# A decoder layer's attention softmax: the bias addition writes negated logits and returns the negated row maximum

## The chip, the cores and the metric

The kernel runs on one core of a Trainium2 chip. A core has five engines with an instruction queue each: TensorE (PE, matrix multiply, with its weight loads shown as PEld), VectorE (DVE), ScalarE (ACT), GpSimd (POOL) and SyncE (SP, which issues most DMAs here). They run side by side and wait for each other through semaphores. The metric is the time of one execution on the device, in microseconds (us).

## What is computed

One layer on 512 tokens of width 1024, in float32: a normalization, one combined projection to q, k, v, two recurrent inputs and two gates, differential attention with 8 heads, a gated linear recurrence beside it, a merge, an output projection, and a squared-ReLU MLP of width 4096. The change is in the softmax of the attention:

```python
logits = jnp.einsum('bqhcd,bkhcd->bhcqk', q_blk, k).astype(jnp.float32) * scale
logits = logits + bias[None, :, None]
logits = jnp.where(rel >= 0, logits, -jnp.inf)
p = jax.nn.softmax(logits, axis=-1)
attn = p[:, :, 0] - lam * p[:, :, 1]
return jnp.einsum('bhqk,bkhe->bqhe', attn.astype(v.dtype), v)
```

Each head has two maps (c = 0 and 1). Each gets a softmax of its own, and the second is subtracted, weighted with lam.

## The kernel before

Every float32 product is made of three matmuls on a high and a low part of each operand. So each weight tile is loaded by DMA (`wraw`), cast by ACT to its high part (`whi`), and DVE subtracts to get the low part (`wlo`). The projection products go to PSUM tiles called `acc`, those of the attention to five shared PSUM tiles called `at`.

The attention runs as 32 steps, 8 heads by 4 blocks of 128 queries; step s has head s // 4 and block i = s % 4, and n = 128 (i + 1) keys. For one step, in this order:

- `logits`: PE makes the two maps' logits (L595), two matmuls each, into two `at` tiles.
- `soft_a`: DVE adds the bias `toep` (which also holds the causal mask) to each map and takes the row maximum in the same instruction. This is one `tensor_tensor_reduce` per map, followed by a small read of the accumulator into `mx`. DVE then makes `nm`, which is `mx` times -1, for both maps at once. ACT takes the exponential of each map with `nm` as bias and sums the rows.
- `soft_b`, one step later: DVE makes the reciprocal `rc` of a row sum, a factor `r2`, and combines the two maps in place (`pe<-pe,r`).
- `turn`, two steps later: PE transposes the combined map, a block of 128 at a time (`ident,pe`, L631). ACT casts the result to its high part `pt`, and DVE subtracts to get the low one (`turn_low`).
- `av`, after every second block: PE multiplies `pt` with `v`.

After each step the loop fills in projection work of the next pair of heads (`qkv_pair`), or of the gates at the end: `acc` matmuls on PE, casts `whi` and squares on ACT, `wlo`, `qn` and `ss` on DVE, and the turning of q and k on PE (`ident,qn`, L529).

The instructions of DVE, ACT and POOL are chained by hand in the order of the program (the wrapper `InOrder`, whose calls all carry line L69). PE in this stage is not: there the framework's scheduler decides how the attention's matmuls and the projections' matmuls follow each other, from its own estimate of when an operand is ready. After the attention come the recurrent branch, the merge and the MLP, which the change does not touch.

Of the kernel before, what the change touches and what calls it, by code (L numbers as in the profile page):

```python
# [13 lines left out]
F32 = mybir.dt.float32  # L14
F32R = mybir.dt.float32r
I32 = mybir.dt.int32
AF = mybir.ActivationFunctionType
ALU = mybir.AluOpType
# [3 lines left out]
P = 128  # L22
# [17 lines left out]
def tile_block(ctx: ExitStack, tc: tile.TileContext, x, w_in, w_rga, w_rgx, w_pa, w_pr, w_o,  # L40
# [7 lines left out]
    sm = ctx.enter_context(tc.tile_pool(name="sm", bufs=4))  # L48
# [28 lines left out]
    V, A, G, T = InOrder(nc.vector), InOrder(nc.scalar), InOrder(nc.gpsimd), nc.tensor  # L77
# [338 lines left out]
    toep = {}  # L416
# [18 lines left out]
    def work(name):  # L435
        return wk.tile([P, S], F32, tag="pe", name=name, bufs=5)
# [144 lines left out]
    def attention(fills, qks, vs, pads):  # L581
        st = {}

        def place(s):
            return s // NT, s % NT
# [12 lines left out]
        def soft_a(s):  # L598
            h, i = place(s)
            n = P * (i + 1)  # L600
            lg = st[s]
            mx = sm.tile([P, 2], F32, tag="mx", name="mx")
            pe = [work("pe") for _ in range(2)]
            for c in range(2):
                V.tensor_tensor_reduce(out=pe[c][:, :n], in0=lg[c][:, :n], in1=toep[h][:, 384 - P * i:512], scale=1.0,
                                       scalar=-3e38, op0=ALU.add, op1=ALU.max, accum_out=mx[:, c:c + 1])
            nm = sm.tile([P, 2], F32, tag="nm", name="nm")
            V.tensor_scalar(out=nm, in0=mx, scalar1=-1.0, scalar2=None, op0=ALU.mult)
            if i == 0:
                st["sums", h] = sm.tile([P, 2, NT], F32, tag="sums", name="sums", bufs=3)  # L610
            sums = st["sums", h]
            for c in range(2):
                A.activation(pe[c][:, :n], pe[c][:, :n], AF.Exp, bias=nm[:, c:c + 1], accum_out=sums[:, c, i:i + 1])
            st[s] = pe

        def soft_b(s):
# [78 lines left out]
        for s in range(NH * NT):  # L695
            h, i = place(s)
            at(s, logits, s)
            at(s, soft_a, s)
            at(s + 1, soft_b, s)
            at(s + 2, turn, s)  # L700
            at(s + 2, turn_low, s)
            if i % 2 == 1:
                at(s + 3, av, s)
            if i == 3:
                at(s + 3, post_a, h)
                at(s + 4, post_b, h)
                at(s + 5, post_c, h)
                at(s + 7, post_d, h)
        for h in range(2, NH):
            at(NT * h - 3, toep_in, h)  # L710
        order = [toep_in, post_c, post_b, av, post_a, turn, logits, soft_a, soft_b, post_d, turn_low]
        for step in sorted(acts):
            j = step // (2 * NT)
# [322 lines left out]
    def task(engine, us, go, after=(), land=None):  # L1036
        t = Task(engine, us, go, [x for x in after if x is not None], AFTER.get(engine, 0.0) if land is None else land)
        for x in t.after:
            x.then.append(t)
        plan.append(t)  # L1040
        return t
# [315 lines left out]
    last_of_chunk, pe, queue, seq = {}, None, {}, []  # L1357
# [3 lines left out]
    def bank_task(key, us, go, after, fresh):  # L1361
        if fresh:
            seq.append(key)
            if len(seq) > 8:
                after = list(after) + queue[seq[-9]]
        else:
            after = list(after) + queue.get(key, [])
        return task("PE", us, go, after)
# [8 lines left out]
    def product_go(o, pairs, u, fresh):  # L1377
        kind, a, p = o
        b, f = (kind, a, BANK.get(p, "Y")), FORM[p]
        split_y = kind == "dn" and a[0] == 3 and b[2] == "Y"  # L1380

        def go():
            if fresh:
                banks[b] = (*banks.get(b, ()), psum("acc")) if split_y else psum("acc")
            hi, lo = units[o]
            if fresh and o in STEADY and u.start == 0:
                first = banks[b][0] if split_y else banks[b]
                x = forms[2 * a[0]][:, 0, f] if kind == "dn" else h2[:, 0, 0, 0:2]
                I.matmul(first[:, :384], hi[:, 0, :P], x.rearrange("p h s -> p (h s)")[:, :384], start=True, stop=True)
            for v in range(u.start, u.stop):  # L1390
                d = banks[b][v][:, :256] if split_y else banks[b][:, 256 * v:256 * v + 256]
                for z, i in enumerate(pairs):
                    for e, (l, r) in enumerate(((hi, 0), (hi, 1), (lo, 0))):
                        act = h2[:, r, i, ACT8[p]] if kind != "dn" else forms[2 * a[0] + i // 2][:, r, f, i % 2]
                        I.matmul(d, l[:, i, P * v:P * v + P], act, start=fresh and z == e == 0 and (v == 0 or split_y),
                                 stop=i == 3 and e == 2, skip_group_check=True)
        return go

    def plain_go(o, half):
        kind, a, p = o  # L1400
        oc, kc = int(p[1]) % 2, int(p[1]) // 2

        def go():
            hi, lo = units[o]
            if kc == half == 0:
                for u in range(2):
                    banks[kind, a, oc, u] = psum("acc")
            for m in range(4 * half, 4 * half + 4):
                u, i = (m // 4, m % 4) if kc else (m % 2, m // 2)
                for e, (l, r) in enumerate(((hi, 0), (hi, 1), (lo, 0))):  # L1410
                    I.matmul(banks[kind, a, oc, u], l[:, i, P * u:P * u + P], h2[:, r, i, 2 * kc:2 * kc + 2], start=kc == i == e == 0, stop=kc == 1 and i == 3 and e == 2)
        return go

    for kind, a, p, pairs in steps:
        o = kind, a, p
        if kind == "pl":
            oc, kc = int(p[1]) % 2, int(p[1]) // 2
            for half in range(2):
                pe = task("PE", 2.73, plain_go(o, half), (pe, lows[o]))
# [4 lines left out]
            if p == "b3":  # L1424
                pe = task("PE", 0.46, norm_go, (pe, norm_split))
# [21 lines left out]
        for u in (slice(0, 1), slice(1, 2)) if split_y else (slice(0, 2),):  # L1447
            key = (*b, u.start) if split_y else b
            pe = bank_task(key, 2.73 * len(pairs) / 4 * (u.stop - u.start) / 2 + 0.17 * (fresh and o in STEADY and u.start == 0), product_go(o, pairs, u, fresh), [pe, *after], fresh)
# [158 lines left out]
```

## Time and profile before

| | us |
|---|---|
| median of 3 runs | 840.35 |
| lowest and highest run | 839.96, 840.93 |
| the profiled execution's own time | 840.35 |
| its span, first to last instruction | 838.6 |
| attention stage, about | 55 to 285 |
| from the recurrent branch on, about | 285 to 838.6 |

The granted clock of TensorE is 1.0 throughout. In the profile's rows, L69 is the line of the wrapper, so instructions of DVE, ACT and POOL are told apart by their tiles: `pe<-at,toep` is the bias addition with its maximum, `mx` the accumulator read, `nm<-mx` the sign change, `pe<-pe,nm` the exponential, `pe<-pe,r` the combining step. "PEld ... [0.45 <-X]" means that the engine stood idle 0.45 us before that instruction and that X ended the wait; "issue" means that the profile names none.

### The profile page before, as it was taken

Reading aid. Unit: us, or ns where it says so; the run is one execution under the profiler, and the core shown is the slowest. Engines: PE = TensorE matmul, PEld = TensorE weight load, DVE = VectorE, ACT = ScalarE, POOL = GpSimd, SP = SyncE. Lnnn points to the kernel's source line nnn. Section 1 sums busy time; section 2 is a strip of 40 time slices with the busy share of each in tenths; the row PEclk is TensorE's granted clock in tenths of the full one; section 3 lists DMA queues with packets and bytes.
Section 4 is the critical chain, followed back from the end, with each engine's and each line's share of the span. In section 5 each row is a group of like instructions: output and inputs, shape, how many; then the busy total and the mean of one; then the engine's idle time right before and its main releaser. Section 6 shows DMA issues by size and latency. Waiting matters only on the chain.

```text
span 838.6 us, 14384 instructions
## 1 busy us (share of the span) xinstructions
PE 832.1 (99%) x5686; PEld 765.0 (91%) x5686; DVE 654.8 (78%) x1077; ACT 478.9 (57%) x753; POOL 104.0 (12%) x132
## 2 busy tenths in 40 slices
PE   9999999999999999999999999999999999999998
PEld 7899999999988887888888888899999999999998
DVE  6776788887877336879766767899989969977996
ACT  7445466555665334685763345774488448645851
POOL 0041231413201101111111000000000000000000
PEclk9999999999999999999999999999999999999999
DMA  6357332433322346667657662355655576556563
GB/s 202 124 153 217 91 110 66 103 123 91 88 77 76 88 138 196 195 189 209 182 170 179 197 253 76 101 151 145 209 151 151 151 256 170 144 164 200 151 168 110
DMA packets 41172, 126.10 MB, mean 150 GB/s; under 512 B 4992, under 2 KB 9800, under 8 KB 41104
## 3 DMA queue, kind: packets, MB, share of 16 engines
q1 hardware_dynamic: 31152, 92.65, 33.6%
q0 software_dynamic: 9952, 32.53, 18.1%
q8 instruction: 45, 0.74, 0.3%
q14 instruction: 23, 0.19, 0.1%
HBM read 102.05 MB, written 11.05 MB: 135 GB/s over the span
## 4 chain that ended last, share of the span: by engine, by line
PE 87%; DVE 5%; DMA 4%; ACT 2%; issue 1%; SPq 0%; ACTq 0%; DVEq 0%
PE acc L69 37%; PE acc L139 14%; PE acc L140 13%; PE acc L141 13%; DMA wraw<-in_w_in_dram 3%; PE at L595 2%; DVE wlo L69 2%; PE at L139 2%; PE at L141 2%; PE at L140 2%; PE at L631 1%; ACT whi L69 1%; PE at L529 1%; DVE pe L69 1%; PE at L668 1%
## 5 line engine op out<-in xcount | busy, mean ns | idle before, releaser
L69 ACT CAST whi<-raw 128x1024 fp32r<-128x1024 f32 x109 | 112.2, 1049 | 93.8 <-DVE raw L69 34.1
L69 DVE TENSOR_TENSOR wlo<-wraw,whi 128x1024 fp32r<-128x1024 f32 (+2 forms) x86 | 96.9, 1148 | 73.7 <-ACT whi L69 73.6
L69 PE MATMUL acc<-us,whi 128*128 128x256 f32 x900 | 153.8, 277 | 0.0
L69 PE MATMUL acc<-h,whi 128*128 128x256 f32 (+1 forms) x851 | 153.7, 285 | 0.0
L69 DVE TENSOR_TENSOR wlo<-raw,whi 128x1024 fp32r<-128x1024 f32 x109 | 131.0, 1218 | 21.0 <-ACT whi L69 20.9
L69 PEld LDWEIGHTS acc<-us,whi 128*128 128x128 f32 x900 | 135.8, 188 | 0.0
L69 PEld LDWEIGHTS acc<-h,whi 128*128 128x128 f32 x851 | 130.7, 188 | 2.6
L69 PE MATMUL acc<-us,wlo 128*128 128x256 f32 x448 | 123.8, 276 | 0.0
L69 PE MATMUL acc<-h,wlo 128*128 128x256 f32 (+1 forms) x424 | 120.6, 285 | 0.0
L69 ACT CAST whi<-wraw 128x1024 fp32r<-128x1024 f32 (+2 forms) x86 | 82.5, 982 | 47.1 <-DMA wraw<-in_w_in_dram 31.6
L139 PE MATMUL acc<-whi,hT 128*128 128x256 f32 x384 | 108.3, 282 | 0.0
L140 PE MATMUL acc<-wlo,hT 128*128 128x256 f32 x384 | 107.1, 279 | 0.2 <-DVE wlo L69 0.2
L69 PEld LDWEIGHTS acc<-us,wlo 128*128 128x128 f32 x448 | 84.1, 188 | 0.0
L139 PE MATMUL acc<-hT,whi 128*128 128x512 f32 x208 | 81.7, 393 | 0.0
L141 PE MATMUL acc<-hT,wlo 128*128 128x512 f32 x208 | 81.2, 390 | 0.0
L69 PEld LDWEIGHTS acc<-h,wlo 128*128 128x128 f32 x424 | 79.6, 188 | 1.3
L141 PE MATMUL acc<-whi,hT 128*128 128x256 f32 x288 | 80.1, 278 | 0.0
L69 ACT ACTIVATE pe<-pe,nm 128x128 f32<-128x128 f32 (+3 forms) x64 | 35.6, 558 | 66.0 <-DVE nm L69 66.0
L140 PEld LDWEIGHTS acc<-wlo,hT 128*128 128x128 f32 x384 | 72.4, 188 | 0.6 <-DVE wlo L69 0.4
L139 PEld LDWEIGHTS acc<-whi,hT 128*128 128x128 f32 x384 | 72.3, 188 | 0.5 <-issue 0.2
L69 POOL TENSOR_TENSOR rs<-ms,mhalf 128x8 f32<-128x8 f32 (+1 forms) x25 | 39.4, 1579 | 187.2 <-DVE ms L69 187.2
L69 POOL DMA_DIRECT2D raw<-raw x24 | 20.7, 863 | 325.7 <-DVE raw L69 117.2
(208 smaller groups left out, 1749.0 us busy)
## 6 DMA issues: line engine op xcount, KB each, us to landing
wraw<-in_w_in_dram SPq DMA_DIRECT2D x54, 512.0 KB, 3.5
raw<-in_w_dn_dram SPq DMA_DIRECT2D x32, 512.0 KB, 4.3
raw<-in_w_up_dram SPq DMA_DIRECT2D x29, 512.0 KB, 4.3
raw<-raw POOLq DMA_DIRECT2D x24, 512.0 KB, 4.6
sum<-in_w_up_dram POOLq DMA_DIRECT2D x18, 512.0 KB, 5.5
wraw<-in_w_pa_dram SPq DMA_DIRECT2D x8, 512.0 KB, 4.7
wraw<-in_w_pr_dram SPq DMA_DIRECT2D x8, 512.0 KB, 4.3
wraw<-in_w_o_dram SPq DMA_DIRECT2D x8, 512.0 KB, 4.2
```

Of the source, the lines that this page charges most:

```text
L69: ins = f(*a, **k)
L139: T.matmul(o, l[0], r[0], start=first, stop=False)
L140: T.matmul(o, l[0], r[1], start=False, stop=False)
L141: T.matmul(o, l[1], r[0], start=False, stop=last)
L529: T.transpose(out=ps[:, t * P:(t + 1) * P], in_=qn[t // 2][:, c0:c0 + P], identity=ident)
L595: T.matmul(lg[c][:, :N], qT[:, c, i * P:(i + 1) * P], qk[h % 2, z][:, c, :N], start=z == 1, stop=z == 2)
L631: T.transpose(out=tp[:, b * P:(b + 1) * P], in_=st[s][:, b * P:(b + 1) * P], identity=ident)
L668: T.matmul(ps[:, t:t + 1], sq[:, t * P:(t + 1) * P], ones, start=True, stop=True)
```

## The change

The bias addition now multiplies its sum by -1 and takes the minimum in place of the maximum, starting at +3e38. What it writes is the negated logit, and what its accumulator holds is the negated row maximum, which is `nm`. The instruction that made `nm` from `mx` is removed. The exponential undoes the sign with a scale of -1. The tile `mx` goes, and `nm` has 8 buffers (`mx` and `nm` had 4 each).

```diff
-            mx = sm.tile([P, 2], F32, tag="mx", name="mx")
+            nm = sm.tile([P, 2], F32, tag="nm", name="nm", bufs=8)
             pe = [work("pe") for _ in range(2)]
             for c in range(2):
-                V.tensor_tensor_reduce(out=pe[c][:, :n], in0=lg[c][:, :n], in1=toep[h][:, 384 - P * i:512], scale=1.0,
-                                       scalar=-3e38, op0=ALU.add, op1=ALU.max, accum_out=mx[:, c:c + 1])
-            nm = sm.tile([P, 2], F32, tag="nm", name="nm")
-            V.tensor_scalar(out=nm, in0=mx, scalar1=-1.0, scalar2=None, op0=ALU.mult)
+                V.tensor_tensor_reduce(out=pe[c][:, :n], in0=lg[c][:, :n], in1=toep[h][:, 384 - P * i:512], scale=-1.0,
+                                       scalar=3e38, op0=ALU.add, op1=ALU.min, accum_out=nm[:, c:c + 1])
...
             for c in range(2):
-                A.activation(pe[c][:, :n], pe[c][:, :n], AF.Exp, bias=nm[:, c:c + 1], accum_out=sums[:, c, i:i + 1])
+                A.activation(pe[c][:, :n], pe[c][:, :n], AF.Exp, scale=-1.0, bias=nm[:, c:c + 1], accum_out=sums[:, c, i:i + 1])
```

On ACT the order stays, but the waits do not. These are ACT's rows around steps 4 and 5 before, with the semaphores that each instruction waits for in brackets (named after the engine that raises them):

```order
L69 ACTIVATE pe,sums<-pe,nm 128x128 [waits DVE_49]
L69 ACTIVATE pe,sums<-pe,nm 128x128 [waits Activation_49]
L69 ACTIVATE qkT<-at,smt 64x512 [waits PE_49]
L69 ACTIVATE qkT<-at,smt 64x512
L69 CAST pt_499<-at 128x4x128 [waits PE_49]
L69 ACTIVATE pe,sums<-pe,nm 128x256 [waits DVE_49]
L69 ACTIVATE pe,sums<-pe,nm 128x256 [waits Activation_49]
```

And these are the same rows of ACT after the change:

```order
L69 ACTIVATE pe,sums<-pe,nm 128x128 [waits DVE_49]
L69 ACTIVATE pe,sums<-pe,nm 128x128 [waits DVE_49,Activation_49]
L69 ACTIVATE qkT<-at,smt 64x512 [waits PE_49]
L69 ACTIVATE qkT<-at,smt 64x512
L69 CAST pt_499<-at 128x4x128 [waits PE_49]
L69 ACTIVATE pe,sums<-pe,nm 128x256 [waits DVE_49]
L69 ACTIVATE pe,sums<-pe,nm 128x256 [waits DVE_49,Activation_49]
```

Before, the first exponential of a pair waits for DVE's `nm`, which covers both maps, and the second needs nothing more of DVE. After, each waits for DVE by itself: the first for the accumulator read of map 0, the second for that of map 1.

On PE, as an example, the place of step 12's transpose (head 3, block 0) behind the turning of q and k (`ident,qn`), before:

```order
L529 MATMUL at<-ident,qn 128x128 x4
L139 MATMUL acc<-whi,hT 128x256
L140 MATMUL acc<-wlo,hT 128x256
L141 MATMUL acc<-whi,hT 128x256
L139 MATMUL acc<-whi,hT 128x256
L140 MATMUL acc<-wlo,hT 128x256
L141 MATMUL acc<-whi,hT 128x256
L139 MATMUL acc<-whi,hT 128x256
L140 MATMUL acc<-wlo,hT 128x256
L141 MATMUL acc<-whi,hT 128x256
L139 MATMUL acc<-whi,hT 128x256
L631 MATMUL at<-ident,pe 128x128
```

The same place on PE after the change, where the lines have moved up by two (L631 is L629):

```order
L529 MATMUL at<-ident,qn 128x128 x4
L139 MATMUL at<-pt_499,v 128x256
L139 MATMUL acc<-whi,hT 128x256
L140 MATMUL acc<-wlo,hT 128x256
L629 MATMUL at<-ident,pe 128x128
```

The transpose followed ten projection matmuls behind the turning, and now follows two and one product with v; the turning itself stands earlier as well. Counted from PE's first row, this transpose moved from row 1077 to row 1041. On DVE the 32 `nm` instructions are gone and nothing else has moved; POOL and SP issue what they issued.

## The prediction

> **What bounds the kernel now.** I read the page first, then the busy time by stage, then the waits of each engine inside the attention stage, and last the timeline around one softmax step.
>
> ```profile
> span 838.6 us, 14384 instructions
> PE 832.1 (99%) x5686; PEld 765.0 (91%) x5686; DVE 654.8 (78%) x1077; ACT 478.9 (57%) x753; POOL 104.0 (12%) x132
> ```
>
> TensorE (PE) is busy nearly all the time, so whatever the change saves on VectorE (DVE) or ScalarE (ACT) counts only where PE stood waiting for them. The changed instructions all lie in the attention stage, about 55 to 285 us:
>
> ```profile
> 55.00:285.00 230.00, 229.45 (x1713) 215.13 (x1713) 174.44 (x463) 126.31 (x276) 54.14 (x54) 1.00 0.37 105
> 525.00:838.60 313.60, 309.61 (x2626) 305.57 (x2624) 273.91 (x327) 191.05 (x252) 20.72 (x24) 1.00 0.58 162
> ```
>
> The columns are the stretch, its length, and busy time with instructions of PE, PE's weight loads (PEld), DVE, ACT and POOL, then the granted clock, the DMA share and GB/s. PE's matmuls overlap, so 229.45 of 230 hides short stalls. They show better in the weight loads, which stop when the next operand is not there. This is who they waited for in the stage:
>
> ```profile
> PEld at L631 <- issue: 1.0, 3, 0.4
> PEld at L452 <- issue: 0.6, 2, 0.3
> PEld at L631 <- DVE pe L69: 0.6, 3, 0.2
> PEld at L139 <- ACT pt L69: 0.5, 2, 0.3
> PEld at L529 <- DVE qn L69: 0.5, 2, 0.3
> PEld at L595 <- issue: 0.5, 2, 0.3
> PEld at L668 <- ACT osq L69: 0.2, 1, 0.2
> PEld acc L139 <- issue: 0.2, 1, 0.2
> PEld at L140 <- DVE pt L69: 0.2, 1, 0.2
> ```
>
> L631 is the transpose of the finished probabilities, L595 the logits, L139 and L140 with pt the product with v, L529 the turning of q and k. Leaving out L452 (the bias table) and the acc row, 1.0 + 0.6 + 0.5 + 0.5 + 0.5 + 0.2 + 0.2 = 3.5 us of PE time hang on DVE and ACT. **That is about all that this change can win**, 0.4% of the time. The largest wait is the transpose's, and it is DVE's doing even where the view says "issue":
>
> ```profile
> 205.47 0.75 DVE L69 SCALAR_TENSOR_TENSOR pe<-pe,r 128x512 f32<-128x512 f32 x1
> 205.70 0.28 PE L140 MATMUL acc<-wlo,hT 128*128 128x256 f32 x1
> 205.81 0.28 PE L141 MATMUL acc<-whi,hT 128*128 128x256 f32 x1
> 206.34 0.31 PEld L631 LDWEIGHTS at<-ident,pe 128*128 128x128 f32 x3 [0.45 <-issue]
> 206.37 0.41 PE L631 MATMUL at<-ident,pe 128*128 128x128 f32 x2 [0.28 <-DVE pe L69]
> ```
>
> Two matmuls of this kind start 0.11 us apart. The transpose starts 0.56 us after the last one, because DVE ended its combining step at 205.47 + 0.75 = 206.22.
>
> **The change, part by part.** First the removed instruction. One step of 128x512 on DVE, then on ACT:
>
> ```profile
> 98.39 0.68 DVE L69 CUSTOM_DVE_ANT_0 pe<-at,toep 128x512 f32<-128x512 f32 x1
> 99.00 0.08 DVE L69 DVE_READ_ACCUMULATOR2_ANT mx<- 128x1 f32 x1
> 99.00 0.69 DVE L69 CUSTOM_DVE_ANT_0 pe<-at,toep 128x512 f32<-128x512 f32 x1
> 99.61 0.08 DVE L69 DVE_READ_ACCUMULATOR2_ANT mx<- 128x1 f32 x1
> 99.72 0.17 DVE L69 TENSOR_SCALAR nm<-mx 128x2 f32<-128x2 f32 x1
> 99.80 0.16 DVE L69 RECIPROCAL rc<-sums 128x1 f32<-128x1 f32 x1
> ...
> 102.42 1.23 DVE L69 TENSOR_TENSOR wlo<-wraw,whi 128x1024 fp32r<-128x1024 f32 x1 [1.15 <-ACT whi L69]
> ```
>
> ```profile
> 99.93 0.72 ACT L69 ACTIVATE pe<-pe,nm 128x512 f32<-128x512 f32 x1 [2.44 <-DVE nm L69]
> ...
> 100.65 0.71 ACT L69 ACTIVATE pe<-pe,nm 128x512 f32<-128x512 f32 x1
> ...
> 101.36 1.03 ACT L69 CAST whi<-wraw 128x1024 fp32r<-128x1024 f32 x1
> ```
>
> From the second read of the accumulator to the reciprocal are 99.80 - 99.61 = 0.19 us. With nm gone the reciprocal can follow the read at once (0.19 saved) or behind its 0.08 (0.11 saved); I take 0.15. There are 32 of them: 4.8 us of DVE, between 3.5 and 6.1.
>
> The larger part is on ACT. Before, both exponentials needed nm, which needed both maxima. After, each carries a wait of its own for its own minimum. nm ended at 99.72 + 0.17 = 99.89 and the exponential began 0.04 later. With the same 0.04 the first can begin at 99.00 + 0.08 + 0.04 = 99.12 instead of 99.93, **0.81 us earlier**. The second follows 0.72 behind it, at 99.84, and by then its own minimum is there (99.61 + 0.08 + 0.04 = 99.73). So the cast behind them moves up by 0.81 too, and with it DVE's wlo at 102.42, which had waited 1.15 for that cast. In the narrowest step the gain is less, about 0.4, since it is one reduction shorter; I take 0.6 as the mean. How much there is to gain shows in these rows, from 85 to 285 us:
>
> ```profile
> ACT pe L69 <- DVE nm L69: 63.6, 28, 3.7
> ...
> ```
>
> ```profile
> DVE wlo L69 <- ACT whi L69: 11.9, 12, 2.2
> ...
> DVE pe L69 <- PE at L595: 7.5, 5, 4.3
> DVE qkT L69 <- ACT qkT L69: 4.4, 3, 1.5
> DVE kl L69 <- ACT qkT L69: 1.8, 3, 0.6
> ```
>
> ACT waits for nm in 28 steps, and DVE waits 18 times (18.1 us) for ACT casts. Those that I looked at stand right behind a pair of exponentials. DVE waits for PE's logits 5 times only, so for most of the stage it trails PE.
>
> Two costs could be new. The reduction now takes the minimum and multiplies by -1 in place of +1, and no row of before shows that form:
>
> ```profile
> L69 DVE TENSOR_TENSOR q<-acc,q 128x512 f32<-128x512 f32 x22 | 14.7, 683 | 0.0
> ...
> L69 DVE CUSTOM_DVE_ANT_0 pe<-at,toep 128x512 f32<-128x512 f32 x16 | 10.4, 688 | 0.0
> ...
> L69 DVE SCALAR_TENSOR_TENSOR pe<-pe,r 128x512 f32<-128x512 f32 x8 | 6.0, 752 | 0.3
> ...
> L69 DVE TENSOR_SCALAR nm<-mx 128x2 f32<-128x2 f32 x32 | 5.4, 169 | 1.1
> ```
>
> The bounds are the plain two-input form (683, 5 ns below the 688 of now) and the one with a further multiply (752, 64 ns above). Over 64 reductions that is -0.3 to +4.1 us of DVE. I take 0, the row of the same instruction, because it multiplied by 1.0 already. The exponential gets a scale of -1:
>
> ```profile
> L69 ACT ACTIVATE pe<-pe,nm 128x512 f32<-128x512 f32 x16 | 11.4, 717 | 26.3 <-DVE nm L69 26.3
> ...
> L69 ACT ACTIVATE tt<-tt,ones 128x512 f32<-128x512 f32 x8 | 5.3, 709 | 0.0
> ```
>
> The second row is an activation with scale -1 and a bias per partition, at 709 against 717: -8 to 0 ns, so I take 0. Both are covered by DVE's and ACT's idle time of the stage anyway (230 - 174.44 and 230 - 126.31); were DVE's cover gone, the 4.1 us would eat up most of the 4.8.
>
> The last part is PE's order. ACT, POOL and SP issue the same sequence as before, and DVE the same without nm. The scheduler, though, places attention's matmuls earlier between those of the projections. Counted by rows at 0.11 us, the transpose of step 7 (head 1) comes 19 rows or 2.1 us earlier, that of step 12 (head 3) 36 rows or 4.0 us, that of step 19 42 rows or 4.6 us, and that of step 9 at the same row. In return projection matmuls come up to 3.5 us later. So PE asks for the probabilities sooner, and DVE must be early enough. I check that at step 12. DVE last waited for PE here:
>
> ```profile
> 93.20 0.56 DVE L69 CUSTOM_DVE_ANT_0 pe<-at,toep 128x384 f32<-128x384 f32 x1 [4.35 <-PE at L595]
> ```
>
> From there to step 12's combining step DVE drops 12 nm (12 x 0.15 = 1.8 us) and passes about six of the 18 waits for ACT (67 of 200 us), each 0.6 shorter (3.6). That is 5.4 against the 4.0 asked, so the transposes should no longer wait.
>
> The sum: the two L631 rows, 1.0 + 0.6 = 1.6 us, go. The other 1.9 us I leave, because they belong to pt, qn and the logits' banks, whose producers are also asked earlier or fed later. The profiled execution took 840.35 us (838.6 us of span and 1.75 around it), which is also the median of the runs shown. 840.35 - 1.6 = 838.75, rounded to **838.8 us**. About 0.2%, or 1.7 us, is what a measurement of this kernel can tell from no change, so this sits at the edge of being seen.
>
> **Rivals.** *All waits go.* If DVE and ACT come early everywhere, the 3.5 us vanish: 836.9. For it speaks that ACT's 63.6 us of waiting for nm is the largest in the stage; against it that a new order brings waits of its own.
>
> *Nothing is gained.* PE's order was laid out anew, and waits of the old size stand at other places; DVE, now earlier, waits for projection results that come up to 3.5 us later. Then the time is 840.35. The 99% of PE speak for it. The Trainium skill, "Perfetto Trace Analysis", section "Identifying the Most-Contended Engine", says to optimize the engine with the highest occupancy first, judging TensorE by its weight loads; with loads at 91% here and DVE at 78%, that rule gives no gain for work taken off DVE.
>
> *Slower.* The transposes stand earlier, but DVE gains only the nm and not the waits for ACT, because projection results arrive later. At step 12 it is then 4.0 - 1.8 = 2.2 us late and PE stands still for that long; later shifts are no larger by more than 0.6, so it is paid about once: 842.5. It decides when DVE's gain up to step 12 falls under 4.0 us. The +4.1 of a slower reduction would push the same way.
>
> That the change doesn't do what it says is hardly open: the nm rows are gone from DVE's order and the second exponential has its own wait.
>
> **Numbers.** Forecast 0.5, spread about 1.2 us to each side (0.3 of it within 0.2%, 0.2 faster); all waits go 0.17, faster; nothing 0.20, same; slower 0.13, of which 0.02 stays within 0.2%. So faster 0.37, same 0.52, slower 0.11. The range from 837.0 to 841.8 holds the forecast and no gain, and reaches into both outer cases.
>
> **What would show it.** Right: no nm on DVE; reductions still near 688 and exponentials near 717 ns; in each step the first exponential starts under 0.2 us behind the first read, so that ACT's wait shrinks by over 10 us; the waits at L631 fall below 0.5 us; the stage ends 1 to 2 us sooner and all later stages last as before. Wrong: waits of the weight loads at the transposes (its new line) of over 2 us, at steps 12 or 19 first; or DVE waiting for projection results; or a reduction over 700 ns.

## The result, and the profile after

| | before | after |
|---|---|---|
| median, us | 840.35 | 836.92 |
| lowest and highest of five runs, us | 839.37, 840.93 | 836.54, 838.28 |
| the profiled execution and its span, us | 840.35, 838.6 | 836.64, 834.9 |

The ratio is 0.9962, with a 95% interval of 0.9951 to 0.9974: about 3.2 us less, 3.4 by the medians. That lies clear of no change. It is at the lower end of the predicted range of 837.0 to 841.8: the ratio makes 837.2 of the 840.35, and the median itself is 0.1 below the range. It stands beside the time of the rival "all waits go" (836.9), not of the forecast (838.8).

First the top of the page of after, and its row of the attention stage from the busy times by stretch (PE, PEld, DVE, ACT, POOL, clock, DMA share, GB/s):

```profile
span 834.9 us, 14382 instructions
PE 828.8 (99%) x5686; PEld 764.1 (92%) x5686; DVE 649.6 (78%) x1045; ACT 479.4 (57%) x753; POOL 103.7 (12%) x132
```

```profile
55.00:285.00 230.00, 229.54 (x1730) 217.37 (x1730) 170.93 (x432) 128.72 (x277) 54.57 (x55) 1.00 0.36 106
```

DVE has 32 instructions fewer (the nm) and 5.2 us less to do. PE still reads 99%, so shares tell nothing here. What tells more is that the same 230 us now hold 1730 matmuls in place of 1713: the stage's work passes sooner.

How much sooner shows in two instructions of PE that every version has: the first logits, and the last transposes. Their timeline rows (start, duration, engine, line), of before and then of after:

```profile
77.67 0.36 PE L595 MATMUL at<-qkT 128*128 128x256 f32 x1
...
273.54 0.60 PE L631 MATMUL at<-ident,pe 128*128 128x128 f32 x4
```

```profile
78.01 0.36 PE L595 MATMUL at<-qkT 128*128 128x256 f32 x1
...
270.44 0.60 PE L629 MATMUL at<-ident,pe 128*128 128x128 f32 x4
```

The difference of the two starts, called the **stage length** from here on, was 195.87 us and is 192.43 us: 3.44 us less. That is most of the 3.71 us between the two profiled executions, and the medians differ by 3.43. Behind 285 us the matmuls of after stand at most 0.9 us sooner than this shift explains, and none stands later; 0.66 of the 0.9 is a pause of PE at 333.4 us that only the profile of before has.

The step that the prediction showed, on DVE and then on ACT, in the timeline of after:

```profile
98.04 0.68 DVE L69 CUSTOM_DVE_ANT_0 pe<-at,toep 128x512 f32<-128x512 f32 x1
98.65 0.08 DVE L69 DVE_READ_ACCUMULATOR2_ANT nm<- 128x1 f32 x1
98.65 0.69 DVE L69 CUSTOM_DVE_ANT_0 pe<-at,toep 128x512 f32<-128x512 f32 x1
99.26 0.08 DVE L69 DVE_READ_ACCUMULATOR2_ANT nm<- 128x1 f32 x1
99.26 0.16 DVE L69 RECIPROCAL rc<-sums 128x1 f32<-128x1 f32 x1
...
101.27 1.23 DVE L69 TENSOR_TENSOR wlo<-wraw,whi 128x1024 fp32r<-128x1024 f32 x1 [0.53 <-ACT whi L69]
```

```profile
98.77 0.73 ACT L69 ACTIVATE pe<-pe,nm 128x512 f32<-128x512 f32 x1 [1.74 <-DVE nm L69]
...
99.49 0.71 ACT L69 ACTIVATE pe<-pe,nm 128x512 f32<-128x512 f32 x1
...
100.19 1.04 ACT L69 CAST whi<-wraw 128x1024 fp32r<-128x1024 f32 x1
```

The first exponential starts 98.77 - 98.65 = 0.12 us behind the first read and overlaps the second reduction. Before, it started 99.93 - 99.00 = 0.93 us behind it, so it is 0.81 us sooner. The reciprocal starts with the second read, where it stood 0.19 behind it before. The cast `whi` ends sooner, so `wlo` waits 0.53 in place of 1.15.

The waits of ACT for these minima (us in total, times, longest), from 85 to 285 us:

```profile
ACT pe L69 <- DVE nm L69: 34.4, 23, 2.9
ACT pt L69 <- PE at L629: 17.4, 13, 4.5
```

63.6 us became 34.4; in return ACT now waits more for PE's transposes (6.8 us before): it comes earlier to them. The waits of PE's weight loads, all rows of the stage:

```profile
PEld at L629 <- DVE pe L69: 0.9, 2, 0.5
PEld at L452 <- issue: 0.6, 2, 0.3
PEld acc L139 <- issue: 0.2, 1, 0.2
PEld at L629 <- issue: 0.2, 1, 0.2
PEld at L139 <- ACT pt L69: 0.2, 1, 0.2
```

Counted as in the prediction (without L452 and the acc row), 3.5 us became 0.9 + 0.2 + 0.2 = 1.3. But the transposes (L629 now) keep 1.1 of their 1.6, while all the others fall from 1.9 to 0.2.

Last the groups of the two changed instructions in their widest shape, and the accumulator read (busy us, mean ns of one, idle time ahead of it):

```profile
L69 ACT ACTIVATE pe<-pe,nm 128x512 f32<-128x512 f32 x16 | 11.4, 717 | 15.5 <-DVE nm L69 15.5
...
L69 DVE CUSTOM_DVE_ANT_0 pe<-at,toep 128x512 f32<-128x512 f32 x16 | 10.4, 687 | 0.2 <-PE at L595 0.2
...
L69 DVE DVE_READ_ACCUMULATOR2_ANT nm<- 128x1 f32 x64 | 5.3, 83 | 0.0
```

687 against 688 and 717 against 717: neither new form costs anything.

### The profile page after: what moved, and what is told of

Read it like the earlier page. It is cut to its first block, busy times and chain, and to the rows that moved or that the text cites. A ratio compares the mean times of both kernels' runs of the same rounds, so it can differ in the third digit from the quotient of the medians.

```text
span 834.9 us, 14382 instructions
## 1 busy us (share of the span) xinstructions
PE 828.8 (99%) x5686; PEld 764.1 (92%) x5686; DVE 649.6 (78%) x1045; ACT 479.4 (57%) x753; POOL 103.7 (12%) x132
## 4 chain that ended last, share of the span: by engine, by line
PE 76%; DVE 10%; ACT 6%; DMA 4%; issue 3%; SPq 0%; ACTq 0%; DVEq 0%
PE acc L69 37%; PE acc L139 10%; PE acc L140 10%; PE acc L141 10%; DVE wlo L69 3%; PE at L595 2%; ACT whi L69 2%; DMA wraw<-in_w_o_dram 2%; DMA wraw<-in_w_pr_dram 2%; PE at L141 1%; PE at L139 1%; PE at L140 1%; PE at L629 1%; DVE gate L69 1%; ACT q L69 1%
## 5 line engine op out<-in xcount | busy, mean ns | idle before, releaser
L139 PE MATMUL acc<-hT,whi 128*128 128x512 f32 x208 | 81.3, 391 | 0.0
L140 PE MATMUL acc<-hT,whi 128*128 128x512 f32 x156 | 60.7, 389 | 0.0
```

The costliest lines, as they stand in the source:

```text
L139: T.matmul(o, l[0], r[0], start=first, stop=False)
L140: T.matmul(o, l[0], r[1], start=False, stop=False)
```

## The experiments

The change brings three things at once, and each could be where the 3.4 us come from:

- **A**: each exponential waits for its own minimum only, so the first starts up to 0.8 us earlier.
- **B**: DVE is rid of the nm instruction.
- **C**: the scheduler laid out PE's matmuls anew.

To part them, PE's order must be held while the rest varies. In the experiments every PE instruction of the attention stage is recorded in a list and chained in a given order. The order of the other engines stays. This part is common to all but the last run:

```diff
+    log = []
+    V, A, G, T = InOrder(nc.vector), InOrder(nc.scalar), InOrder(nc.gpsimd), Logged(nc.tensor)
...
+        for a, b in zip(order, order[1:]):
+            tc.add_manual_dep(log[b], log[a].name, ORDER, reason="order")
```

`Logged` passes every call on and notes the instruction; `order` is the sequence of either kernel. In these traces PE's rows all carry line L86 and the other engines' L70. Stage lengths are worked out as above, from the two rows of each run's one profiled execution. Each ratio is to runs of before on the same chip (their median is 840.80 us for e1 to e4, 840.52 for e5, e6, e7 and e1b):

| | A, B, order | median us | ratio to before | stage length us |
|---|---|---|---|---|
| before | -, -, old | 840.35 | 1 | 195.87 |
| e8, before again | -, -, old | 843.11 (one run) | | 195.82 |
| after | A, B, new | 836.92 | 0.9962 [0.9951, 0.9974] | 192.43 |
| e7, order held | A, B, new | 837.92 | 0.9964 [0.9950, 0.9979] | 192.67 |
| e1 | A, B, old | 836.33 | 0.9945 [0.9931, 0.9960] | 192.01 |
| e1b, the same again | A, B, old | 837.75 | 0.9961 [0.9947, 0.9975] | 192.51 |
| e6 | A, -, old | 837.34 | 0.9958 [0.9942, 0.9974] | 192.22 |
| e5 | -, B, old | 839.11 | 0.9978 [0.9966, 0.9990] | 192.94 |
| e4 | A, -, new | 838.98 | 0.9978 [0.9968, 0.9988] | 194.20 |
| e3 | -, B, new | 842.84 | 1.0028 [1.0015, 1.0041] | 197.83 |
| e2 | -, -, new | 845.28 | 1.0056 [1.0043, 1.0070] | 201.25 |

The stage length repeats better than the time: before twice 195.87 and 195.82, after and its held copy 192.43 and 192.67, e1 and e1b 192.01 and 192.51. So differences over 0.5 us can be read from it. The total of a profiled execution is no such measure: that of e3 (841.13) is the fastest of its twelve runs, and that of e5 (841.18) the slowest of its twelve.

**e1: the changed kernel with PE's old order.** Nothing else differs from the changed kernel.

> The changed kernel, with PE's matmuls of the attention stage held in the order that they have before the change. Three theories: A, the gain of 3.4 us comes from the exponentials that start 0.4 to 0.8 us sooner on ACT; B, it comes from the 0.19 us that each missing nm saves on DVE (6.1 us in all); C, it comes from PE's re-laid order. A and B: DVE is earlier and the old order asks no sooner, so the waits at the transposes go and the time is 836.5 to 838. C: nothing is left of the gain, 840 to 840.6.

The ratio is 0.9945 and the median 836.33, a little under the 836.5 to 838 that A and B gave, and the stage length is 192.01. The waits of its weight loads in the stage:

```profile
PEld at L86 <- issue: 0.6, 2, 0.3
PEld at L86 <- ACT osq L70: 0.2, 1, 0.2
PEld acc L86 <- issue: 0.2, 1, 0.2
```

The 0.6 is the bias table's, as in both kernels (L452 there), so 0.2 us is left of 3.5. The gain is there in full without the new order. C isn't its source.

**e2: the kernel before with the new order.**

> The kernel before, with PE's matmuls of the attention stage in the order that they have after the change. A and B: PE asks for the probabilities up to 4.6 us sooner while DVE and ACT are as late as before, so PE waits at the transposes of steps 7 to 20 and the time is 841 to 843 (the forecast's slower rival said 842.5). C: the order alone brings the gain, 836.5 to 838.

The ratio is 1.0056, and the stage is 201.25 - 195.87 = 5.4 us longer. The median of 845.28 is over the 841 to 843 that A and B gave. The waits of its weight loads:

```profile
PEld at L86 <- issue: 4.7, 7, 1.4
PEld at L86 <- DVE pe L70: 1.9, 5, 0.7
PEld at L86 <- DVE qkT L70: 1.8, 3, 0.8
PEld at L86 <- ACT pt L70: 0.5, 1, 0.5
PEld at L86 <- DVE pt L70: 0.5, 1, 0.5
PEld at L86 <- PE acc L86: 0.4, 1, 0.4
PEld at L86 <- DVE qn L70: 0.2, 1, 0.2
```

Without the bias table's 0.6 they are 9.4 us against 3.5. Of these, 5.0 stand at the transposes, and 3.1 at the logits, 1.8 of them put down to DVE's `qkT`, which the expectation had not counted. The longest at the transposes are those of steps 11, 12 and 19, in the timeline of the weight loads:

```profile
155.85 0.42 PEld L86 LDWEIGHTS at<-ident,pe 128*128 128x128 f32 x4 [0.99 <-issue]
...
160.15 0.14 PEld L86 LDWEIGHTS at<-ident,pe 128*128 128x128 f32 x1 [0.69 <-DVE pe L70]
...
207.32 0.42 PEld L86 LDWEIGHTS at<-ident,pe 128*128 128x128 f32 x4 [1.35 <-issue]
```

The new order alone is a loss: it asks for the probabilities, and for q and k, before the old DVE has them.

**e3: the changed kernel without A.** The two exponentials change places, so that the first one needs the minimum that comes last. The nm instruction stays away.

```diff
-            for c in range(2):
+            for c in (1, 0):
                 A.activation(pe[c][:, :n], pe[c][:, :n], AF.Exp, scale=-1.0, bias=nm[:, c:c + 1], accum_out=sums[:, c, i:i + 1])
```

> The changed kernel in its own order, but with the two exponentials of a step swapped, so that the first one needs the last reduction and the early start on ACT is lost; nm stays away from DVE. A: the gain is mostly lost and the order asks too early, 840 to 842. B: 836.5 to 838, as the changed kernel. C: 837 to 838.

On the step shown above, the first exponential now starts 99.28 - 98.49 = 0.79 us behind the first read:

```profile
98.49 0.08 DVE L70 DVE_READ_ACCUMULATOR2_ANT nm<- 128x1 f32 x1
...
99.28 0.72 ACT L70 ACTIVATE pe<-pe,nm 128x512 f32<-128x512 f32 x1 [2.31 <-DVE rc L70]
```

It was 0.93 before and 0.12 after, so 0.67 of the 0.81 us are taken back; the rest comes with the missing nm. The ratio is 1.0028, slower than before, and the median of 842.84 is a little over what A gave. The first rows of its weight loads' waits, and three of their places (steps 11, 12 and 19):

```profile
PEld at L86 <- issue: 2.8, 5, 0.9
PEld at L86 <- DVE pe L70: 1.2, 3, 0.6
PEld at L86 <- DVE qkT L70: 1.2, 2, 0.8
PEld at L86 <- PE at L86: 0.8, 1, 0.8
```

```profile
153.97 0.42 PEld L86 LDWEIGHTS at<-ident,pe 128*128 128x128 f32 x4 [0.86 <-issue]
...
158.12 0.14 PEld L86 LDWEIGHTS at<-ident,pe 128*128 128x128 f32 x1 [0.61 <-DVE pe L70]
...
203.95 0.42 PEld L86 LDWEIGHTS at<-ident,pe 128*128 128x128 f32 x4 [0.82 <-PE at L86]
```

Under the new order, A is worth 197.83 - 192.55 = 5.3 us of the stage (192.55 is the mean of after and e7). B alone isn't enough for this order. Without the bias table and the acc row, PE's listed waits are 5.9 us: 3.2 at the transposes, 2.5 at the logits and 0.2 at the product with v.

**e4: the changed kernel without B.** An instruction of nm's shape is put back where nm stood; nobody reads its result. `nm` has 4 buffers again.

```diff
+            mx = sm.tile([P, 2], F32, tag="mx", name="mx")
+            V.tensor_scalar(out=mx, in0=nm, scalar1=-1.0, scalar2=None, op0=ALU.mult)
```

> The changed kernel in its own order, with an instruction of nm's size and wait put back on DVE whose result nobody reads; the exponentials still start early. A: 837 to 838, as the changed kernel. B: 840 to 842. C: 837 to 838.

The ratio is 0.9978: the stage is 1.7 us longer than in the full change, and still 1.7 shorter than before. The median of 838.98 lies between what A alone (837 to 838) and B alone (840 to 842) gave, so under this order both count. ACT's wait for the minima stays short, which shows that A is kept:

```profile
ACT pe L70 <- DVE nm L70: 35.6, 24, 2.9
```

**e5 and e6: B alone and A alone, under the old order.** The edits are those of e3 and e4.

> The changed kernel with PE's old order and the exponentials swapped, so only nm is missing against the kernel before. The runs so far ruled out C as a gain. Together: the early start of the exponentials (A) is worth about 5.5 us under the new order and nm's time on DVE (B) about 1.3. Under the old order the most that can be won is the 3.5 us of waits: with B alone 838.5 to 839.5 us if the two add up, 837 or less if either suffices.

> The changed kernel with PE's old order and an instruction of nm's size put back on DVE: only the early start of the exponentials is left. If A is the larger part, 836.5 to 837.5 us and at most 0.5 us of waits at the transposes; if both parts are needed, 838 to 839.

The stage lengths are 192.94 (B alone) and 192.22 (A alone) against some 192.3 for both (e1, e1b). Either one nearly suffices, and both medians (839.11 and 837.34) are as expected. In e5 the listed waits that are left are 0.7 us, for `pt` and `osq`. The instruction put back does run in e6 and costs what nm did (169 ns before):

```profile
L70 DVE TENSOR_SCALAR mx<-nm 128x2 f32<-128x2 f32 x32 | 5.6, 176 | 1.1
```

Yet of the waits of PE's weight loads it brings back only this one:

```profile
PEld at L86 <- DVE pe L70: 0.2, 1, 0.2
```

**e7 and e1b: the new and the old order, side by side.** e7 is the changed kernel with its own order held, as a control of the method; e1b repeats e1.

> The changed kernel with its own order of PE held by the same means as the old order is held in the others: a control. 836.5 to 838 us, as the changed kernel; anything else would mean that the way of holding the order costs time itself.

> The changed kernel with PE's old order again, beside the control on the same chip: 1.0 to 2.0 us below the control if the old order is better for it, since the control's weight loads still waited 1.3 us for DVE and ACT and this one's 0.2.

Holding the order changes nothing by itself: 0.9964 against 0.9962. But the old order doesn't bring the 1 to 2 us over the control that were expected after e1: it is 0.2 us by the medians, with intervals that overlap. Over both pairs the stage is 192.26 under the old order and 192.55 under the new one. If the new order costs anything inside the full change, it is about 0.3 us, which these runs can't tell from nothing.

**e8: the kernel before, profiled a second time.**

> The kernel before, a second profile. The first showed PE standing still for 0.66 us at 333.4 us (first product of the recurrent gates), which none of the other profiles did. If it belongs to the kernel it is there again; if it is scatter of one execution, it is gone, and so are 0.7 us of the difference between the two spans. The waits for DVE and ACT in the attention stage should be 3 to 4 us again. 840 to 841 us.

The stage is 195.82 us long, as in the first profile, so its lengths can be compared between runs. The pause at 333.4 us is gone, so it was scatter of one execution. But the listed waits are not the 3 to 4 us that were expected. Counted as before they are 2.7 us, and the transposes have 1.1 of them, not 1.6:

```profile
PEld at L631 <- issue: 0.9, 3, 0.4
...
PEld at L631 <- DVE pe L69: 0.2, 1, 0.2
```

At the same stage length, the list of waits thus differs by 0.8 us between two executions of one kernel. The whole execution took 843.11 us (a second run of before on this chip 841.43), not 840 to 841: its matmuls fall back by 2.4 us between 345 and 500 us, in code that no version here touches. A single execution's total is therefore no measure of a 3 us effect; the medians and the stage length are.

**What they add up to.** Read by the order, the stage is:

| stage length, us | neither | B alone | A alone | both |
|---|---|---|---|---|
| old order | 195.87, 195.82 | 192.94 | 192.22 | 192.01, 192.51 |
| new order | 201.25 | 197.83 | 194.20 | 192.43, 192.67 |

Both rows end at about 192 us, however far they started from it. There the listed waits of PE are nearly gone (0.2 us in e1, 1.3 in after). A and B don't add under the old order: B alone wins 2.9 us, A alone 3.6, and both together 3.6, after which there is next to no listed wait left to win. Under the new order the stage starts from 201.25 us, and the full change needs both (3.4 and 7.1 alone, 8.7 together).

## Why the prediction was right or wrong

**The stage and the cap held.** All of the gain lies in the attention stage, and it is of the size of the waits of PE on DVE and ACT (3.5 us) that the prediction named as about all that could be won. The stage lost 3.44 us. The forecast itself was half of that: 838.8 against 836.92. "Faster", which came true, had a chance of 0.37, and "same" 0.52; that the range held the result at its lower end owes to its width, which reached toward the rival.

**The costs taken as zero were zero**: the reduction at 687 ns and the exponential at 717.

**The early exponential** starts 0.12 us behind the first read (forecast: under 0.2), and ACT's wait shrank by 29 us (forecast: over 10). That it is 0.81 us sooner is just what the prediction worked out. DVE's waits for the casts of ACT hardly shrank, though: the three rows that the prediction added up to 18.1 us come to 17.5 after. DVE came sooner to these waits as well, and it now waits for PE's logits 9 times in place of 5.

**The saving per nm** was the upper bound. The prediction chose 0.15 between 0.11 and 0.19; the rows show 0.19, in all 32 steps, so 6.1 us of DVE time and not 4.8. Under the old order this had little weight, since A alone brought the whole gain there; under the new one all of B is worth 1.7 us.

**The size was off, at one step: "the two L631 rows, 1.0 + 0.6 = 1.6 us, go. The other 1.9 us I leave".** It came out the other way round. The transposes kept 1.1 of 1.6 us (the prediction's sign was under 0.5; e8's profile of before has 1.1), and the waits for pt, qn, osq and the logits' banks fell from 1.9 to 0.2 (1.6 in e8). The reason given for leaving them ("whose producers are also asked earlier or fed later") overlooked that those producers are DVE and ACT too: whatever lets these engines run ahead of PE brings pt, qn and osq sooner as well as the combined map. e1 shows it under the old order, where 0.2 us of all waits is left.

The listed waits lost 3.5 - 1.3 = 2.2 us, and the stage 3.44. The rest is in pauses that the view of waits doesn't list. For the 1460 spacings between matmul starts in the stage, take what each is above the median of its kind over all these runs. Spacings that are over 95 ns too long then add up to 3.0 us before (2.4 in e8) and 1.3 after, and those that are 20 to 95 ns too long to 6.2 us before (6.2 in e8) and 4.6 after. Together that is 3.3 us less (2.7 from e8). So about half of the gain lies in pauses that the listed 3.5 us hardly hold, and that the 3.5 came out so close to the gain is in part luck. Why the short pauses shrink was not traced.

**"5.4 against the 4.0 asked, so the transposes should no longer wait"** was off on both sides. These are step 12's combining steps, before and then after:

```profile
159.58 0.35 DVE L69 SCALAR_TENSOR_TENSOR pe<-pe,r 128x128 f32<-128x128 f32 x1
```

```profile
155.19 0.35 DVE L69 SCALAR_TENSOR_TENSOR pe<-pe,r 128x128 f32<-128x128 f32 x1
```

From the first logits (77.67 and 78.01) to their ends are 82.26 and 77.53 us, so DVE gained 4.7 us there and not 5.4. Worked out alike, B alone gained 1.4 us (e3; the prediction had 1.8) and A alone 3.8 (e4; 3.6). And 4.7 is over the 4.0 asked, yet the transpose waited 0.35 us: PE came to it 4.7 + 0.35 = 5.1 us sooner (an estimate; before, the transpose started 0.06 us behind the combining step), more than its 36 rows at 0.11 us make. These are the weight loads of after that still wait for the combining step, at steps 11, 12 and 20 in the timeline:

```profile
151.72 0.42 PEld L629 LDWEIGHTS at<-ident,pe 128*128 128x128 f32 x4 [0.18 <-issue]
...
155.60 0.14 PEld L629 LDWEIGHTS at<-ident,pe 128*128 128x128 f32 x1 [0.35 <-DVE pe L69]
...
204.32 0.14 PEld L629 LDWEIGHTS at<-ident,pe 128*128 128x128 f32 x1 [0.50 <-DVE pe L69]
```

DVE gained enough for nearly all of what the new order asks, and is a few tenths of a microsecond short at three places. So the 1.1 us that the transposes kept are waits of a new order, not remains of the old ones.

**The rivals.** "All waits go" gave the right time, 836.9, though 1.3 us of listed waits are left: the short pauses that went make up for them, so its number is right in part by luck. "Nothing is gained" falls with an interval that ends at 0.9974. Its argument, PE's 99%, says nothing about the 1% in which the gain lay. The Trainium skill, "Perfetto Trace Analysis", section "Identifying the Most-Contended Engine", says which engine to optimize first; that work taken off another one brings no gain was the prediction's reading of it, and the measured ratio of 0.9962 speaks against that reading here.

"Slower" did not happen, but its mechanism is real. e3 is that case: the transposes stand earlier and DVE gains the nm but not the early exponentials. It was priced at 842.5 and took 842.84, and that agreement is in part luck. The rival had one wait of 2.2 us at step 12. e3 waits 0.61 there, 0.86 and 0.82 at steps 11 and 19, less at other transposes, and 2.5 us at the logits, which the rival left out. What decided between this rival and the forecast was the size of A, and there the prediction was right: 3.6 us of DVE's gain up to step 12 by its working, 3.8 by e4.

**What stays open.** Why the old and the new order give the same time with A and B in place, within 0.3 us, was only measured, not traced wait by wait. Nor was the spread between 345 and 500 us looked into.

## What to carry to other kernels

Where one engine is busy 99% of the time, add up what that engine waits for in the stage that a change touches, and look at the short pauses between its instructions too. Here the listed waits (3.5 us, 2.7 in a second profile) gave the size of the gain. If the edit speeds up all the producers, expect to get most of it rather than the rows that name the edited tile. Ask of an edit not only which instruction goes, but which operand is there sooner: splitting a wait for both halves into one wait for each was worth more than the removed instruction (3.6 against 2.9 us under the old order, each alone). And since a scheduler may re-lay the order of the bound engine for a small edit (here alone 5 us of the stage to the bad), hold that order fixed to see what the edit itself is worth.

## What the runs showed of the hardware

- The accumulator read (83 ns busy) takes no time of its own from the next instruction: the second reduction is recorded at 98.65 with the first read, and the reciprocal at 99.26 with the second, and so it is in all 32 steps. A removed instruction of 169 ns that read the accumulator's result gave back 0.19 us from start to start.
- Minimum with a factor of -1 in the fused reduction takes as long as maximum with +1 (687 and 688 ns at 128x512), and the exponential with scale -1 as long as with 1 (717 and 717).
- Two profiles of the same kernel agreed to 0.05 us over 196 us of the attention stage, and differed by 2.4 us over the 155 us between 345 and 500 us.
